# Linear attention's values and decayed keys: block transposes on VectorE and transfers through device memory in the place of 64 TensorE transposes

## The chip, the cores and the metric

The kernel runs on one core of a Trainium2 chip, as one program from its first instruction to its last. The metric is the device time of one execution in microseconds. A core has a matrix engine (TensorE, PE in the profile), a vector engine (VectorE, DVE), a scalar engine (ScalarE, ACT), GpSimd (POOL) and SyncE (SP), which here only issues transfers. The engines work side by side, each through its own list in order, and wait for each other through semaphores. TensorE writes its results to PSUM, from where another engine fetches them.

## The reference

One step of a decoder layer for 256 tokens of a prompt and 8 x 4 tokens of samples, 288 in all, in float32. The layer projects the normalized input, runs two branches of attention, merges them, and ends with a feed-forward part:

```python
h = rms_norm(x, norm1)
z = h @ w_in                      # all projections in one
qs, ks, vs, qg, kg, vg, rg, ag, gs, gg = split(z)
o_swa = sliding_window_attention(...)
o_g, S_new = gla_recurrent(qg * 256 ** -0.5, kg, vg, log_a, S0)
o_g = o_g * rsqrt(mean(o_g * o_g) + EPS) * gla_norm * silu(rg)
y = sigmoid(gs) * (o_swa @ p_swa) + sigmoid(gg) * (o_g @ p_gla)
x = x + y @ w_o
x = x + square(relu(rms_norm(x, norm2) @ w_up)) @ w_down
```

What matters here is the linear attention `gla_recurrent`: 4 heads, keys of 256 features, values of 512. With the running sum `b` of the logarithm of the forget gates inside a chunk of tokens,

```python
q_i, k_i, k_d = q * exp(b), k * exp(-b), k * exp(b_last - b)
o = causal(q_i @ k_i.T) @ v + q_i @ S
S = exp(b_last) * S + k_d.T @ v
```

The state `S` of each head (256 x 512) is an output, one for the prompt and one for each of the 8 samples.

## The kernel before

Activations lie with features on the 128 partitions and the 288 tokens along the free axis. A projection is done by `gemm` (L220 to L253): weights come in chunks of 512 KB (`raw`, 6 buffers, loaded by SP at L231), ScalarE casts each half to a reduced float (`whi`, L216), VectorE takes the rest (`wlo`, by the helper at L156), 5 buffers each, and TensorE does 24 matmuls for each chunk (L249): hi by hi, hi by lo and lo by hi. 520 chunks follow each other in the order of `ORDER`.

Everything else is laid into this stream in small steps. `gla(h)` and `gla_sample(h)` are generators, put into two queues by `start_head(h)`; after each chunk `pump` takes some steps from each queue (rates 1.0 or 0.9, and 0.7). A `yield` ends a step. The written order is only a priority: a planner lays the instructions of each engine out by the times that it models, and keeps the written order where `keep_in_program_order` asks for it. On the chip each engine then works through its list strictly in order, SP's list of transfers too.

A head's projections `qk{h}` and `v{h}` fill `zqk[h]` and `zv[h]` (features on partitions). For the products with tokens as the summed axis, values and decayed keys are needed the other way round, tokens on partitions. `gla(h)` does this on TensorE:

- values of the prompt: for each of 2 blocks of 128 tokens, 4 transposes of 128x128 into the PSUM bank `pv` (L679) and a copy by ScalarE into `vt` (tile `vtok`, L680). From `vt` come `vh` and `vl`, the halves of the split values, which enter the products for the output (`po`, L806 to L809) and the state (`pst`, L823 to L826).
- decayed keys: `kd` for each half `t` of the 256 features (L725 is the last of its operations), then 2 x 2 transposes into the bank `pk` (L778), a cast by ScalarE into `kdt` (L779) and the remainders `kdl` by VectorE. They enter the state's products.
- the state's products of the last head are done at the end of the kernel from `vt` and `kdt`, which are kept till then.

`gla_sample(h)` turns the 32 tokens of the samples: 4 transposes into `pvs` (L840), a copy into `vf` (L841) and a write of `vf` to the device memory `vd` (L842). `vf` is used in products of the samples' output (L885); `vd` is read back much later by `state_updates`, broadcast to all partitions (`vb`, L1035). Between these steps `gla_sample` loads the samples' old states, 4 and then 4 more, into buffers of the same pool `raw` as the weights (L867), and multiplies them (`pos`, L892).

That makes 8 + 4 + 4 = 16 transposes for each head, 64 in all, in groups of four.

The tile pools matter for the order: tiles with the same tag share their buffers, and a new one waits until the readers of the old are done. `vt` shares its tag with `w2r`, the small weights that the head loads at its start (L655); `kdl` shares with `kd`, `kdt` with a part of the gates (tag B); tag F holds the tiles `ob` and `sqo` of `gla_sample`; the tags `Za0` to `Zb3` of the pool `main` hold the large tiles of the heads.

Of the kernel before, what the change touches and what calls it, by code (L numbers as in the profile page):

```python
# [12 lines left out]
F32 = mybir.dt.float32  # L13
# [6 lines left out]
P = 128  # L20
D = 2048
KT = 16
TP = 256
NB = 8
NS = 4
TS = NB * NS
NT = TP + TS
# [7 lines left out]
QS, KS, VS_, QG, KG, VG, RG, AG, GS, GG = OFF[:10]  # L35


def w_in_groups():

    ar = np.arange  # L40
    g = {}
    g["kv"] = np.concatenate([ar(KS, KS + 256), ar(VS_, VS_ + 256)])
    for p in range(2):
        cols = []
        for r in range(4):
            for u in range(2):
                h = (2 * p + u) * 4 + r
                cols.append(ar(QS + h * 64, QS + h * 64 + 64))
        g[f"q{p}"] = np.concatenate(cols)
    for i in range(4):  # L50
        g[f"gs{i}"] = ar(GS + i * 512, GS + i * 512 + 512)
        g[f"gg{i}"] = ar(GG + i * 512, GG + i * 512 + 512)
        g[f"rg{i}"] = ar(RG + i * 512, RG + i * 512 + 512)
        g[f"qk{i}"] = np.concatenate([ar(QG + i * 256, QG + i * 256 + 256), ar(KG + i * 256, KG + i * 256 + 256)])
        g[f"v{i}"] = ar(VG + i * 512, VG + i * 512 + 512)
    return g


def swa_rows():

    rows = []
    for p in range(2):
        for r in range(4):
            for u in range(2):
                h = (2 * p + u) * 4 + r
                rows.append(np.arange(h * 64, h * 64 + 64))
    return np.concatenate(rows)
# [64 lines left out]
def step_kernel(ctx: ExitStack, tc: tile.TileContext, a: dict):  # L132
# [7 lines left out]
    def f(ap):  # L140
        return ap.bitcast(F32)

    def bank(name):
        return psm.tile([P, 512], F32, name=name, tag="sm")

    def flat(ap):
        return ap.rearrange("p a b -> p (a b)")
# [7 lines left out]
    def sub(out, x, y, eng=V):  # L155
        eng.tensor_tensor(out, x, y, ALU.subtract)  # L156


    ident = main.tile([P, P], F32, name="ident")
# [472 lines left out]

    dec = gpool.tile([P, 4, 2, NB], F32, name="dec")
    kdk = gpool.tile([P, 4, 2, TS], F32, name="kdk")
    vd = ctx.enter_context(tc.tile_pool(name="values", bufs=1, space=bass.MemoryType.DRAM)).tile([4, TS, 512], F32, name="vd")
    V.memset(qm, 0.0)
    wsel, wsgn = bm[:, 64 + NB:65 + NB], bm[:, 65 + NB:66 + NB]

# [10 lines left out]

    def gla(h):  # L650
        zq, zk = (lambda t: zqk[h][:, t]), (lambda t: zqk[h][:, 2 + t])
        yield
        w2r = gpool.tile([P, 256], F32, name="w2r", tag="vtok")
        w2 = gpool.tile([P, 256], F32R, name="w2")
# [19 lines left out]

        vt = gpool.tile([P, 2, 512], F32, name="vtok", tag="vtok")
        for blk in range(2):
            pv = bank("pv")
            for j in range(4):
                T.transpose(pv[:, P * j:P * j + P], zv[h][:, j, P * blk:P * blk + P], ident)  # L679
            S.copy(vt[:, blk], pv)  # L680
            yield
        o_g = og[h] = main.tile([P, 4, NT], F32, name=f"og{h}", tag=f"Zb{h}")

        kds, ee, ees = [], [], []
        for t in range(2):
            e = main.tile([P, 9, P], F32, name="e", tag=f"Za{2 + t}")
            en = gpool.tile([P, 2, P], F32, name="en", tag="en", bufs=2)
            kd = gpool.tile([P, 2, P], F32, name="kd", tag="kd", bufs=2)
            tot = gpool.tile([P, 1], F32, name="tot", tag="tot", bufs=2)
            cs = gpool.tile([P, 2, 6], F32, name="cs", tag="cs", bufs=2)  # L690

            px = pfx[:, t, 0:TP].rearrange("p (a b c) -> p a b c", a=2, c=32)
            end = px[:, :, :, 31]

            add(cs[:, :, 0:5:4], end[:, :, 0:4:2], end[:, :, 1:4:2])
            V.tensor_copy(cs[:, :, 1:6:4], end[:, :, 1:4:2])
            add(cs[:, :, 2:4], cs[:, :, 0:2], cs[:, :, 4:5].broadcast_to([P, 2, 2]))
            S.activation(tot, cs[:, 1, 2:3], AF.Exp, scale=GATE)
            runs = lambda i: e[:, i:i + 2].rearrange("p a (b c) -> p a b c", c=32)
            far, l64, dg, l32 = runs(0), runs(2), runs(4), runs(7)  # L700
            sub(far, cs[:, :, 2:6].unsqueeze(3).broadcast_to([P, 2, 4, 32]), px)
            sub(l64[:, :, 0:2], cs[:, :, 0:2].unsqueeze(3).broadcast_to([P, 2, 2, 32]), px[:, :, 0:2])
            V.tensor_copy(l64[:, :, 2], px[:, :, 2])
            add(l64[:, :, 3], px[:, :, 3], end[:, :, 2:3].broadcast_to([P, 2, 32]))
            yield
            sub(dg, px, px[:, :, :, 15:16].broadcast_to([P, 2, 4, 32]))
            sub(l32[:, :, 0:4:2], end[:, :, 0:4:2].unsqueeze(3).broadcast_to([P, 2, 2, 32]), px[:, :, 0:4:2])
            V.tensor_copy(l32[:, :, 1:4:2], px[:, :, 1:4:2])
            running(e[:, 6], ones, las[t][:, P:TP])
            S.activation(flat(en), flat(e[:, 4:6]), AF.Exp, scale=-GATE)  # L710
            S.activation(flat(e), flat(e), AF.Exp, scale=GATE)
            yield
            q2 = zq(t)[:, 0:TP].rearrange("p (a b) -> p a b", a=2)
            k2 = zk(t)[:, 0:TP].rearrange("p (a b) -> p a b", a=2)
            mul(e[:, 0], e[:, 0], k2[:, 0])
            mul(e[:, 6], e[:, 6], q2[:, 1])
            mul(e[:, 2:4, 0:64], e[:, 2:4, 0:64], k2[:, :, 0:64])
            mul(e[:, 2:4, 64:P], e[:, 2:4, 64:P], q2[:, :, 64:P])
            for i, x in ((0, k2), (32, q2)):
                e5 = e[:, 7:9].rearrange("p a (b c) -> p a b c", b=2)[:, :, :, i:i + 32]  # L720
                mul(e5, e5, x.rearrange("p a (b c) -> p a b c", b=2)[:, :, :, i:i + 32])
            mul(e[:, 4:6], e[:, 4:6], q2)
            mul(en, en, k2)
            mul(kd[:, 1], e[:, 1], k2[:, 1])
            V.tensor_scalar(kd[:, 0], e[:, 0], tot, None, ALU.mult)  # L725
            kds.append(kd)
            yield
            ee.append(e)
            ees.append(en)
        pa = bank("pa")  # L730
        V.memset(pa[:, :448], 0.0)

# [39 lines left out]
        yield  # L772
        parts = h < 3
        kdt = gpool.tile([P, 2, 256], F32R if parts else F32, name="kdt", tag="B")
        pk = bank("pk")
        for blk in range(2):
            for t in range(2):
                T.transpose(pk[:, 256 * blk + P * t:256 * blk + P * t + P], kds[t][:, blk], ident)  # L778
        S.copy(flat(kdt), pk)  # L779
        if parts:  # L780
            kdl = [gpool.tile([P, 256], F32R, name="kdl", tag="kd", bufs=2) for _ in range(2)]
            for blk in range(2):
                sub(kdl[blk], pk[:, 256 * blk:256 * blk + 256], f(kdt[:, blk]))
            vh = main.tile([P, 2, 512], F32R, name="vh", tag="tt")
            vl = []
            for blk in range(2):
                S.copy(vh[:, blk], vt[:, blk])
                for c in (slice(0, 256), slice(256, 512)):
                    lo = main.tile([P, 256], F32R, name="vl", tag=("zr", "sr")[blk], bufs=2)
                    sub(lo, vt[:, blk, c], f(vh[:, blk, c]))  # L790
                    vl.append(lo)
                yield
            ath, atl = (gpool.tile([P, 256], F32R, name=n) for n in ("ath", "atl"))
            S.copy(ath, at[0])
            sub(atl, at[0], f(ath))
            yield
# [35 lines left out]
    def gla_sample(h):  # L832
# [2 lines left out]
        ps = ready[h][:, :, TP:NT]  # L835

        vf = gpool.tile([TS, 512], F32, name="vf")
        pv = bank("pvs")
        for j in range(4):
            T.transpose(pv[:TS, P * j:P * j + P], zv[h][:, j, TP:NT], ident)  # L840
        S.copy(vf, pv[:TS])  # L841
        SY.dma_start(vd[h], vf)  # L842
        yield
        ps4 = ps.rearrange("p a (b c) -> p a b c", c=NS)
        es = gpool.tile([P, 2, 64], F32, name="es")
# [183 lines left out]
    def state_updates():  # L1029
# [2 lines left out]

        def load_values(i):
            h, b = items[i]
            SY.dma_start(vb[:, i % 2], vd[h, 4 * b:4 * b + 4].rearrange("a b -> (a b)").unsqueeze(0).broadcast_to([P, 2048]))  # L1035
        load_values(0)

        paced = tc.keep_in_program_order
# [128 lines left out]
def lay_out(i):  # L1167
# [3 lines left out]
    m["x"] = np.ascontiguousarray(x.T.reshape(KT, P, NT).transpose(1, 0, 2))  # L1171
    feat = lambda v: v.reshape(-1, P).T
    m["xn"] = np.concatenate([feat(i["norm1"][0]), m["x"][:, 0]], axis=1)
    m["norms"] = np.concatenate([feat(i["norm2"][0]), feat(i["final_norm"]), feat(i["gla_norm"][0])], axis=1)
    w_in = i["w_in"][0]
    parts = {n: pack(w_in[:, c])[0] for n, c in w_in_groups().items()}
    for n, w in (("ps", i["p_swa"][0][swa_rows()]), ("pg", i["p_gla"][0]), ("wo", i["w_o"][0])):
        p = pack(w)
        for j in range(4):
            parts[f"{n}{j}"] = p[j]  # L1180
# [13 lines left out]
    ck, cv = i["cache_swa_k"][0], i["cache_swa_v"][0]  # L1194
    m["kc"] = np.ascontiguousarray(ck.reshape(NB, P, 2, P).transpose(2, 3, 0, 1))
    m["vc"] = np.ascontiguousarray(cv.reshape(NB, P, 2, P).transpose(2, 1, 0, 3))
    s0 = i["state_gla"][0]
    m["s0"] = np.ascontiguousarray(s0.reshape(NB, 4, 2, P, 512).transpose(1, 0, 3, 2, 4)).reshape(4, NB, P, 1024)
    return {k: np.ascontiguousarray(v) for k, v in m.items()}

# [38 lines left out]
```

## Time and profile before

| | us |
|---|---|
| median of 3 runs | 1745.99 |
| lowest and highest run | 1745.26, 1748.83 |
| span of the profiled execution, first to last instruction | 1748.4 |
| weight chunks: TensorE's time for 24 matmuls, from the chain | 3.15 to 3.17 |
| transposes of the change: first and last start | 223.7, 633.6 |

The profile gives no other time of its own execution than the span, which lies within those of the three runs. A line of the groups names the line of the program, the engine, the operation, the tiles (result, then operands), the shapes and the count; behind the bar stand the busy time of all, the mean length of one in ns, and the time that the engine was idle just before them, with those who ended that wait. The chain is followed back from the last instruction, at each step to what released it or to the instruction before it on its engine. "SPq" is SP's own list of transfers.

### The profile page before, as it was taken

The numbers are of one execution on the slowest core, as the hardware profiler recorded it, in microseconds if no ns is written. First come the engines' busy times: TensorE is split into PE (matmuls) and PEld (weight loads), VectorE is DVE, ScalarE is ACT, GpSimd is POOL, SyncE is SP. The second block draws the span as 40 slices with busy tenths as digits, with TensorE's granted clock in tenths as the row PEclk, the third lists the DMA queues.
The fourth block names the chain that finished last, engine by engine and source line by source line (L and its number), as shares of the span: only waits on it lengthen the run. The fifth ranks groups of instructions, "written<-read, shape, count | busy, mean of one in ns | idle before, by whom it ended". The sixth has DMA issues, their size and how long they took to land.

```text
span 1748.4 us, 34547 instructions
## 1 busy us (share of the span) xinstructions
PE 1737.7 (99%) x13491; PEld 1710.8 (98%) x13491; DVE 1207.2 (69%) x2312; ACT 890.9 (51%) x1681; POOL 2.9 (0%) x12
## 2 busy tenths in 40 slices
PE   9999999999999999999999999999999999999997
PEld 8999999999999999999999999999999999999997
DVE  8896575665745656666678777777777777777555
ACT  6555465444534645544556554455544554455543
POOL 0000000000000000000000000000000000000000
PEclk9999999999999999999999999999999999999999
DMA  8645456456464465555866677776777677765552
GB/s 302 212 138 181 136 171 220 169 191 208 158 246 159 147 229 169 185 167 166 320 217 235 235 268 252 275 255 249 255 247 283 239 240 281 267 240 210 176 178 92
DMA packets 102883, 374.74 MB, mean 214 GB/s; under 512 B 12480, under 2 KB 15040, under 8 KB 98624
## 3 DMA queue, kind: packets, MB, share of 16 engines
q1 hardware_dynamic: 102144, 371.49, 60.5%
q8 instruction: 105, 1.72, 0.4%
q10 hardware_dynamic: 576, 1.05, 0.2%
q14 instruction: 58, 0.48, 0.1%
HBM read 348.58 MB, written 23.92 MB: 213 GB/s over the span
## 4 chain that ended last, share of the span: by engine, by line
PE 99%; DVE 0%; DMA 0%; ACT 0%; issue 0%; DVEq 0%
PE mm L249 94%; PE pos L892 1%; PE score L458 0%; PE o L502 0%; PE pt L490 0%; PE po L806 0%; PE os L582 0%; DVE x L150 0%; PE po L809 0%; DMA raw<-in_w 0%; PE pv L679 0%; PE pa L734 0%; PE pst L825 0%; PE pst L823 0%; PE pst L826 0%; PE ssq L258 0%
## 5 line engine op out<-in xcount | busy, mean ns | idle before, releaser
L156 DVE TENSOR_TENSOR wlo<-raw,whi 128x512 fp32r<-128x512 f32 x1040 | 703.0, 688 | 455.3 <-ACT whi L216 449.8
L216 ACT CAST whi<-raw 128x512 fp32r<-128x512 f32 x1040 | 630.8, 619 | 721.1 <-PE mm L249 660.9
L249 PE MATMUL mm<-hh,whi 128*128 128x288 f32 x1472 | 436.3, 297 | 0.1
L249 PE MATMUL mm<-hl,whi 128*128 128x288 f32 x1472 | 431.4, 294 | 0.0
L249 PE MATMUL mm<-hh,wlo 128*128 128x288 f32 x1472 | 429.4, 292 | 0.0
L249 PE MATMUL mm<-uh,whi 128*128 128x288 f32 x1024 | 301.1, 294 | 0.0
L249 PE MATMUL mm<-ul,whi 128*128 128x288 f32 x1024 | 301.1, 294 | 0.0
L249 PE MATMUL mm<-h2h,whi 128*128 128x288 f32 x1024 | 301.1, 294 | 0.0
L249 PE MATMUL mm<-h2l,whi 128*128 128x288 f32 x1024 | 301.1, 294 | 0.0
L249 PE MATMUL mm<-uh,wlo 128*128 128x288 f32 x1024 | 300.7, 294 | 0.0
L249 PE MATMUL mm<-h2h,wlo 128*128 128x288 f32 x1024 | 300.7, 294 | 0.0
L249 PEld LDWEIGHTS mm<-hh,whi 128*128 128x128 f32 x1472 | 276.2, 188 | 5.9 <-issue 3.0
L249 PEld LDWEIGHTS mm<-hl,whi 128*128 128x128 f32 x1472 | 276.1, 188 | 0.3
L249 PEld LDWEIGHTS mm<-hh,wlo 128*128 128x128 f32 x1472 | 276.0, 188 | 0.0
L249 PEld LDWEIGHTS mm<-uh,wlo 128*128 128x128 f32 x1024 | 193.2, 189 | 0.0
L249 PEld LDWEIGHTS mm<-h2h,wlo 128*128 128x128 f32 x1024 | 193.2, 189 | 0.0
L249 PEld LDWEIGHTS mm<-uh,whi 128*128 128x128 f32 x1024 | 192.4, 188 | 0.0
L249 PEld LDWEIGHTS mm<-h2h,whi 128*128 128x128 f32 x1024 | 192.4, 188 | 0.0
L249 PEld LDWEIGHTS mm<-h2l,whi 128*128 128x128 f32 x1024 | 191.8, 187 | 0.0
L249 PEld LDWEIGHTS mm<-ul,whi 128*128 128x128 f32 x1024 | 191.8, 187 | 0.0
L1047 DVE SCALAR_TENSOR_TENSOR acc_s<-vb,kdk,acc_s 128x512 f32<-128x512 f32 x192 | 142.2, 745 | 0.4
L249 PE MATMUL mm<-yl,whi 128*128 128x288 f32 x256 | 75.2, 294 | 0.0
(290 smaller groups left out, 1778.1 us busy)
## 6 DMA issues: line engine op xcount, KB each, us to landing
raw<-in_w SPq DMA_DIRECT2D x518, 512.0 KB, 3.9
vb<-vd SPq DMA_DIRECT2D x32, 1024.0 KB, 6.9
raw<-in_s SPq DMA_DIRECT2D x32, 512.0 KB, 4.2
old<-in_s SPq DMA_DIRECT2D x32, 512.0 KB, 4.2
out_ssn<-old SPq DMA_DIRECT2D x32, 512.0 KB, 5.2
x<-in_x SPq DMA_DIRECT2D x4, 576.0 KB, 6.5
x<-in_x SPq DMA_DIRECT2D x6, 288.0 KB, 7.1
out_y<-x SPq DMA_DIRECT2D x6, 288.0 KB, 2.7
```

The lines of the kernel that those rows point to most:

```text
L156: eng.tensor_tensor(out, x, y, ALU.subtract)
L216: S.copy(hi, raw)
L249: T.matmul(o, lhsT=(lo if j == 2 else hi)[:, sl], rhs=xl(k) if j == 1 else xh(k), start=k == 0 and j == 0, stop=k == nk - 1 and j == 2)
L892: T.matmul(pos[r:r + 32], lhsT=qm[:, t, 32 * b:32 * b + 32], rhs=st[i + g][:, 512 * t:512 * t + 512], start=b < 2, stop=b >= NB - 2)
L1047: paced(V.scalar_tensor_tensor(acc[t], v(n), k(n), acc[t], ALU.mult, ALU.add))
```

## The change

Each head's values and decayed keys are turned by VectorE in blocks of 32x32. Such an operation turns each block in its place, so that a tile of 128 features by 288 tokens becomes, in each group of 32 partitions, 9 blocks of 32 tokens by 32 features. The groups are put together by writes to device memory: the group of 32 partitions `g` writes its features into its own columns, and reading back rows of tokens gives tokens on partitions.

- `gla(h)` has a new first step: four block transposes into `vtb` (in the buffer `Za2`), four writes of the samples' block to `vd[h]` and four of the prompt's eight blocks to `vtd[h]`. In the place of transposes and copies, two loads fill `vt` from `vtd[h]`.
- for each half `t` of the keys a block transpose goes into `ktb` (tag F), then four writes to `kdd[h]`. Later two loads fetch the turned keys: for the first three heads into the two tiles `kdl`, from which, one step later, ScalarE casts `kdt` and VectorE takes the remainder in place; for the last head directly into `kdt`.
- `gla_sample(h)` loads `vf` from `vd[h]`; its transposes, the copy and the write of `vf` go.
- the features of a head come in another order this way (`VALUES`, `KEYS`). The gate's columns `rg`, the rows of `p_gla`, `gla_norm` and the old states are laid out in that order on the host, and the states are put back in the old order on the host when the kernel is done.

```diff
+def blocks_turned(n):
+    return np.arange(32 * 4 * n).reshape(n, 4, 32).transpose(1, 0, 2).ravel()
+VALUES, KEYS = blocks_turned(4), blocks_turned(2)
...
-        g[f"rg{i}"] = ar(RG + i * 512, RG + i * 512 + 512)
+        g[f"rg{i}"] = RG + i * 512 + VALUES
...
-    vd = ctx.enter_context(tc.tile_pool(name="values", bufs=1, space=bass.MemoryType.DRAM)).tile([4, TS, 512], F32, name="vd")
+    dram = ctx.enter_context(tc.tile_pool(name="values", bufs=1, space=bass.MemoryType.DRAM))
+    vd = [dram.tile([TS, 512], F32, name=f"vd{h}") for h in range(4)]
+    vtd = [dram.tile([NB, 32, 512], F32, name=f"vtd{h}") for h in range(4)]
+    kdd = [dram.tile([NB, 32, 256], F32, name=f"kdd{h}") for h in range(4)]
...
     def gla(h):
         zq, zk = (lambda t: zqk[h][:, t]), (lambda t: zqk[h][:, 2 + t])
+        yield
+        vtb = main.tile([P, 9, 4, 32], F32, name="vtb", tag="Za2")
+        for m in range(4):
+            V.transpose(vtb[:, :, m], zv[h][:, m].rearrange("p (t c) -> p t c", c=32))
+        for g in range(4):
+            rows_ = vtb[32 * g:32 * g + 32].rearrange("p t m c -> p t (m c)")
+            cols = slice(P * g, P * g + P)
+            SY.dma_start(vd[h][:, cols], rows_[:, 8])
+            SY.dma_start(vtd[h][:, :, cols].rearrange("t a x -> a t x"), rows_[:, 0:8])
         yield
...
         for blk in range(2):
-            pv = bank("pv")
-            for j in range(4):
-                T.transpose(pv[:, P * j:P * j + P], zv[h][:, j, P * blk:P * blk + P], ident)
-            S.copy(vt[:, blk], pv)
+            SY.dma_start(vt[:, blk], vtd[h][4 * blk:4 * blk + 4].rearrange("t a x -> (t a) x"))
             yield
...
-        kds, ee, ees = [], [], []
+        ee, ees = [], []
+        ktb = gpool.tile([P, NB, 2, 32], F32, name="ktb", tag="F")
...
-            kds.append(kd)
+            V.transpose(ktb[:, :, t], flat(kd).rearrange("p (b c) -> p b c", c=32))
             yield
             ee.append(e)
             ees.append(en)
+        for g in range(4):
+            SY.dma_start(kdd[h][:, :, 64 * g:64 * g + 64].rearrange("t a x -> a t x"),
+                         ktb[32 * g:32 * g + 32].rearrange("p b t c -> p b (t c)"))
...
-        pk = bank("pk")
-        for blk in range(2):
-            for t in range(2):
-                T.transpose(pk[:, 256 * blk + P * t:256 * blk + P * t + P], kds[t][:, blk], ident)
-        S.copy(flat(kdt), pk)
         if parts:
             kdl = [gpool.tile([P, 256], F32R, name="kdl", tag="kd", bufs=2) for _ in range(2)]
+        for blk in range(2):
+            SY.dma_start(f(kdl[blk]) if parts else kdt[:, blk], kdd[h][4 * blk:4 * blk + 4].rearrange("t a x -> (t a) x"))
+        if parts:
+            yield
             for blk in range(2):
-                sub(kdl[blk], pk[:, 256 * blk:256 * blk + 256], f(kdt[:, blk]))
+                S.copy(kdt[:, blk], f(kdl[blk]))
+                sub(kdl[blk], f(kdl[blk]), f(kdt[:, blk]))
...
         vf = gpool.tile([TS, 512], F32, name="vf")
-        pv = bank("pvs")
-        for j in range(4):
-            T.transpose(pv[:TS, P * j:P * j + P], zv[h][:, j, TP:NT], ident)
-        S.copy(vf, pv[:TS])
-        SY.dma_start(vd[h], vf)
+        SY.dma_start(vf, vd[h])
...
-            SY.dma_start(vb[:, i % 2], vd[h, 4 * b:4 * b + 4].rearrange("a b -> (a b)").unsqueeze(0).broadcast_to([P, 2048]))
+            SY.dma_start(vb[:, i % 2], vd[h][4 * b:4 * b + 4].rearrange("a b -> (a b)").unsqueeze(0).broadcast_to([P, 2048]))
```

More of the change, by code (lines that the diff above doesn't have):

```diff
@@ L1173, in lay_out @@
     m["xn"] = np.concatenate([feat(i["norm1"][0]), m["x"][:, 0]], axis=1)
-    m["norms"] = np.concatenate([feat(i["norm2"][0]), feat(i["final_norm"]), feat(i["gla_norm"][0])], axis=1)
+    m["norms"] = np.concatenate([feat(i["norm2"][0]), feat(i["final_norm"]), feat(i["gla_norm"][0][VALUES])], axis=1)
     w_in = i["w_in"][0]
     parts = {n: pack(w_in[:, c])[0] for n, c in w_in_groups().items()}
-    for n, w in (("ps", i["p_swa"][0][swa_rows()]), ("pg", i["p_gla"][0]), ("wo", i["w_o"][0])):
+    for n, w in (("ps", i["p_swa"][0][swa_rows()]), ("pg", i["p_gla"][0].reshape(4, 512, D)[:, VALUES].reshape(D, D)), ("wo", i["w_o"][0])):
         p = pack(w)
@@ L1196, in lay_out @@
     m["vc"] = np.ascontiguousarray(cv.reshape(NB, P, 2, P).transpose(2, 1, 0, 3))
-    s0 = i["state_gla"][0]
+    s0 = i["state_gla"][0][..., VALUES]
     m["s0"] = np.ascontiguousarray(s0.reshape(NB, 4, 2, P, 512).transpose(1, 0, 3, 2, 4)).reshape(4, NB, P, 1024)
@@ L1231 @@
     vc = o["vcn"].transpose(2, 1, 0, 3).reshape(NB, P, 4, 64)
-    sp = o["sp"].reshape(1, 1, 4, 256, 512)
-    ss = o["ssn"].reshape(4, NB, P, 2, 512).transpose(1, 0, 3, 2, 4).reshape(1, NB, 4, 256, 512)
+    vo, ko = np.argsort(VALUES), np.argsort(KEYS)
+    sp = o["sp"].reshape(1, 1, 4, 256, 512)[:, :, :, ko][..., vo]
+    ss = o["ssn"].reshape(4, NB, P, 2, 512).transpose(1, 0, 3, 2, 4).reshape(1, NB, 4, 256, 512)[..., vo]
     c = np.ascontiguousarray
```

## The prediction

> **What bounds the kernel now.** I read the page first: the busy time of each engine and the chain of work that ended last.
>
> ```profile
> PE 1737.7 (99%) x13491; PEld 1710.8 (98%) x13491; DVE 1207.2 (69%) x2312; ACT 890.9 (51%) x1681; POOL 2.9 (0%) x12
> ...
> PE 99%; DVE 0%; DMA 0%; ACT 0%; issue 0%; DVEq 0%
> ```
>
> TensorE (PE) is busy 99% of the span and 99% of the chain is TensorE. So the end comes when TensorE's list is worked off: what leaves that list shortens the run, and what is added elsewhere costs only where it makes TensorE wait. The average hides stages, so next come the busy times in the four stretches in which the four heads of the linear attention run beside the projections (columns: stretch, its length, busy time and instructions of PE, PEld, DVE, ACT, POOL, then granted clock, DMA share, GB/s).
>
> ```profile
> 205.00:315.00 110.00, 110.00 (x907) 105.17 (x906) 64.91 (x150) 58.82 (x106) 0.70 (x2) 1.00 0.53 187
> 315.00:430.00 115.00, 115.00 (x930) 111.03 (x930) 72.83 (x165) 54.50 (x103) 0.66 (x2) 1.00 0.55 188
> 430.00:545.00 115.00, 115.00 (x935) 111.03 (x935) 69.45 (x156) 53.41 (x100) 0.66 (x2) 1.00 0.55 190
> 545.00:660.00 115.00, 115.00 (x933) 111.19 (x932) 70.08 (x156) 59.77 (x109) 0.66 (x2) 1.00 0.54 187
> ```
>
> All 64 transposes of the change lie in these stretches. TensorE has no gap in any of them, VectorE (DVE) is idle 42 to 46 us of each, ScalarE (ACT) 51 to 62 us, and the transfers use some 55% of the DMA engines. Busy time alone would mislead, because matmuls overlap. What a transpose takes from the chain is read in the chain itself, here between 205 and 330 us, head 0 (start, length, what, how many):
>
> ```profile
> 223.84 0.44 PE pvs L840 x4
> ...
> 236.89 0.44 PE pv L679 x4
> ...
> 276.25 0.44 PE pk L778 x4
> ...
> 278.89 12.80 PE mm L249 x96
> ```
>
> Four transposes stand together each time, and each group holds the chain for 0.44 us, whichever of the three kinds it is. A head has four such groups: one `pvs`, two `pv`, one `pk`.
>
> **The change part by part.** The groups by line hold what goes, the nearest relatives of what comes, and the two steps that prepare the weights (after the count: busy in all, mean ns of one, idle time before and who ended it):
>
> ```profile
> L156 DVE TENSOR_TENSOR wlo<-raw,whi 128x512 fp32r<-128x512 f32 x1040 | 703.0, 688 | 455.3 <-ACT whi L216 449.8 <-PE pk L778 3.9
> L216 ACT CAST whi<-raw 128x512 fp32r<-128x512 f32 x1040 | 630.8, 619 | 721.1 <-PE mm L249 660.9 <-DMA raw<-in_w 38.3 <-ACT whi L216 8.5
> ...
> L249 PEld LDWEIGHTS mm<-hh,whi 128*128 128x128 f32 x1472 | 276.2, 188 | 5.9 <-issue 3.0 <-ACT whi L216 1.6 <-ACT kdt L779 0.8
> ...
> L648 DVE TENSOR_TENSOR_SCAN pfx<-seg,ls 128x288 f32<-128x288 f32 x8 | 5.6, 739 | 0.0
> ...
> L679 PE MATMUL pv<-ident,zv 128*128 128x128 f32 x32 | 4.8, 272 | 0.0
> ...
> L396 DVE STREAM_SHUFFLE rot<-swa_q 128x288 f32<-128x288 f32 x8 | 3.6, 480 | 0.0
> ...
> L840 PE MATMUL pvs<-ident,zv 128*32 128x128 f32 x16 | 2.4, 272 | 0.0
> L778 PE MATMUL pk<-ident,kd 128*128 128x128 f32 x16 | 2.4, 272 | 0.0
> ```
>
> *TensorE.* 32 + 16 + 16 = 64 transposes in 16 groups. At 0.44 us each they give back **16 x 0.44 = 7.0 us**. The 272 ns of one in its row is its length from start to end; on the chain four follow each other 0.11 us apart, so the rows' 64 x 0.272 = 17.4 us is an upper end that I don't take. The Trainium skill, page "TensorE: Matmul & The Clock Gate", Part 4, gives some 275 ns for a transpose inside a kernel: the trace's 272 ns agrees as a duration, but a sum of 64 such durations would promise 17.6 us where the chain shows 7.0.
>
> *ScalarE* loses the copies of the turned values out of PSUM, three in each head; for three heads the one cast of the keys becomes two of half its width, and the fourth head's goes. It is off the chain and idle almost half of each stretch: nothing either way.
>
> *VectorE* gains, for each head, four block transposes of 128x288 and two of 128x256. The trace of before has none. The nearest row is the shuffle of 128x288, 480 ns, which also moves elements between partitions; the scan of that size, 739 ns, is my upper end, and below nothing there is no reason to go. With 480 ns: 4 x 0.48 + 2 x 0.48 x 256/288 = 2.8 us a head, 11.1 us in all (17.1 by the scan). A burst of 1.9 us delays the `wlo` step that stands behind it. What hides this: VectorE is idle 455.3 us before those steps, mostly waiting for ScalarE's casts, and ScalarE's casts waited 660.9 us for TensorE to free a buffer. The preparation of weights runs ahead of TensorE, so I cost it at nothing; if the cover were gone, it would cost the 11.1 us.
>
> *SP's queue.* Per head come 8 writes of the turned values, 1 + 2 loads of them, 4 writes and 2 loads of the keys; the write of `vd` from `vf` goes: 16 more. Issue and landing times (first SP's own instructions with min/median/max ns, then KB each and median us to landing):
>
> ```profile
> L231 SPq DMA_DIRECT2D raw<-in_w x512: 327/328/1973, 18.0 to 1710.4; - x171
> ```
>
> ```profile
> raw<-in_w SPq DMA_DIRECT2D x518, 512.0 KB, 3.9
> vb<-vd SPq DMA_DIRECT2D x32, 1024.0 KB, 6.9
> ...
> w2r<-in_w SPq DMA_DIRECT2D x4, 128.0 KB, 2.7
> ...
> vd<-vf SPq DMA_DIRECT2D x4, 64.0 KB, 1.6
> ```
>
> 16 x 0.33 = 5.2 us of issuing in a head of 115 us. The bytes are small: per head about 0.6 MB of values and 0.25 MB of keys, written once and read once, against 512 KB for every single chunk of weights. What matters is order: SP works its list in sequence, and the new loads wait until the writes they read back have landed, while the weight loads stand behind them. Both waits are new, `vtd` to `vt` and `kdd` to `kdt`. SP's waits as they are (who for whom: us in total, times, longest):
>
> ```profile
> SPq L231 <- DVE wlo L156: 1069.6, 417, 8.4
> ```
>
> SP spends 1069.6 us waiting for a free weight buffer, so weights are normally asked for as early as the buffers allow. The values have time: they are written when the head begins and their first use in `vh` lies several chunks later. The thin place is behind the second four state loads. There (SP, ScalarE and VectorE in order of time, head 0: start, length, what):
>
> ```profile
> 267.86 28.62 SPq L231 DMA_DIRECT2D raw<-in_w  x13
> ```
>
> ```profile
> 275.87 1.90 ACT L216 CAST whi<-raw 128x512 fp32r<-128x512 f32 x3 [2.92 <-DMA raw<-in_w]
> ```
>
> ```profile
> 276.52 1.97 DVE L156 TENSOR_TENSOR wlo<-raw,whi 128x512 fp32r<-128x512 f32 x3 [5.47 <-ACT whi L216]
> ```
>
> A load issued at 267.86 is cast at 275.87; its first `wlo` part is done at 276.52 + 0.69 = 277.2, and the chain above begins with these weights at 278.89. The cover is 1.7 us, and 1.2 us once the `pk` group is out of the way. I take the same cover for the other heads. If the keys' loads were late just here, ScalarE's new copy of `kdl` would hold the casts behind it. The price per head is the landing less 1.2 us: 2.7 - 1.2 = 1.5 us by the load of the same 128 KB (`w2r`), 3.9 - 1.2 = 2.7 us by a weight load; three heads have that copy, so 0 to 8.1 us. Below nothing: the 0.8 us for which TensorE waited on `kdt` may go. Which end is nearer follows from when the keys are ready:
>
> ```profile
> 245.07 0.28 DVE L725 TENSOR_SCALAR kd<-e,tot 128x128 f32<-128x128 f32 x1
> ```
>
> I take **+0.5 us**, near the lower end, since in head 0 the last product that is turned ends at 245.35, about 30 us before this place: the two block transposes and the landings of the write and the load (1.6 and 2.7 us) fit in between.
>
> The extra steps of the head's list (one at its start, one after the keys' loads) move its work by a chunk; TensorE has projections to do meanwhile: nothing.
>
> **The sum.** -7.0 + 0.5 = -6.5 us, 0.37%. The profiled span is 1748.4 us, within the runs (1745.26 to 1748.83) and 2.4 above their median; I take the difference over to the median: 1745.99 - 6.5 = **1739.5 us**. About 0.2%, 3.5 us, is what a measurement of this kernel can tell from no change, so faster means below 1742.5 and slower above 1749.5.
>
> **The rivals.**
> - *Given back at the landings* (the same): the copy of `kdl` waits in ScalarE's order at the thin place. With 1.5 us in three heads 1745.99 - 7.0 + 4.5 = 1743.5, with 2.7 us 1747.0. For it: the cast there already waits 2.92 us for a transfer. Against it: the keys are early in head 0.
> - *SP holds the weights back* (slower): the keys' loads stand in SP's list ahead of weight loads at the thin place, and SP waits for the landing of `kdd`. By the only read-back that the trace has, 6.9 us, it costs 4 x (6.9 - 1.2) = 22.8 us: 1761.8. It decides from 10.5 us lost in all, that is a hold of 2.6 + 1.2 = 3.8 us in each head. Against it: the 1069.6 us show SP ahead of the work, waiting for buffers far more than for results, and the keys' loads can be asked for while it waits for one.
> - *VectorE becomes the bound* (slower): its 11.1 us land on the path: 1745.99 - 7.0 + 11.1 = 1750.1. Against it: 42 us idle in each stretch. The Trainium skill, page "VectorE: DVE Perf Modes", section "Rules for kernel authors", advises TensorE for a 128x128 transpose whose result may go to PSUM, which speaks against the change; it goes by the single operation, and the rows say which engine has time to spare.
> - *Full durations are saved* (faster): 1745.99 - 17.4 = 1728.6. Against it: the 0.44 us of each group in the chain.
> - *The change doesn't shorten TensorE's run* (the same): the transposes filled time in which weights were not ready, and TensorE now waits instead: 1746. Against it: only 5.9 us of idle time before the largest group of weight loads in 1472 of them.
>
> **Chances.** Forecast 0.68; given back 0.18; SP holds back 0.08; VectorE 0.02; full durations 0.02; no shorter 0.02. So faster 0.68 + 0.02 = 0.70, the same 0.18 + 0.02 = 0.20, slower 0.08 + 0.02 = 0.10. The range: at the low end the full 7.0 us and the 0.8 us of waiting, from the fastest run, 1745.26 - 7.8 = 1737.5, rounded down to 1737.0; at the top the dearer form of the first rival, 1747.0, rounded up to 1747.5. That leaves out the last slower and faster cases, some 0.12, and a little of the forecast's edges.
>
> **What the profile after would show.** Right: no `pv`, `pvs` and `pk` groups; some 64 fewer TensorE instructions, no new piece in the chain in their place; block transposes near 0.48 us with VectorE's busy time up by some 11 us; ScalarE's some us lower; the idle time before `mm` weight loads as small as now. Wrong: `mm` loads that wait for `whi` or `wlo` right after the keys' loads (first two rivals), or SP's waits on `vtd` or `kdd` of over 4 us each with weight loads behind them.

## The result, and the profile after

| | us |
|---|---|
| before, median of 4 runs (lowest, highest) | 1746.56 (1745.26, 1748.83) |
| changed, median of 4 runs (lowest, highest) | 1739.91 (1738.3, 1740.5) |
| ratio, with its 95% interval | 0.9961 (0.9949 to 0.9972) |
| profiled execution of the changed kernel: time, span | 1738.3, 1736.6 |

The change takes 6.65 us off, 0.38%. The page of the changed kernel, busy times and shares of the chain:

```profile
PE 1725.7 (99%) x13427; PEld 1699.0 (98%) x13427; DVE 1213.8 (70%) x2336; ACT 884.7 (51%) x1671; POOL 2.9 (0%) x12
...
PE 99%; DVE 1%; DMA 0%; ACT 0%; issue 0%; DVEq 0%
```

13491 - 13427 = 64 instructions have left TensorE, and 99% of the chain is still TensorE. That fits a run that got shorter because TensorE's list did; the experiments have to show it. The four stretches of the heads, in the columns of the prediction:

```profile
205.00:315.00 110.00, 110.00 (x904) 105.42 (x903) 67.22 (x158) 58.06 (x105) 0.72 (x2) 1.00 0.60 203
315.00:430.00 115.00, 115.00 (x927) 111.11 (x927) 74.80 (x171) 53.12 (x100) 0.65 (x2) 1.00 0.62 208
430.00:545.00 115.00, 115.00 (x933) 111.11 (x933) 71.90 (x164) 53.36 (x101) 0.65 (x2) 1.00 0.61 205
545.00:660.00 115.00, 115.00 (x932) 111.26 (x931) 73.46 (x163) 58.84 (x106) 0.66 (x2) 1.00 0.62 206
```

TensorE has no gap in any of them. VectorE is busy 2 to 3 us more in each, and the transfers use 60 to 62% of the DMA engines where they used 53 to 55%. The chain in head 0, at the places where the groups `pvs`, `pv` and `pk` stood:

```profile
210.78 15.75 PE mm L257 x120
226.53 0.26 PE pl L686 x2
226.79 37.83 PE mm L257 x288
...
268.45 9.45 PE mm L257 x72
277.90 0.35 PE pos L902 x8
278.25 1.85 PE pos L909 x16
280.10 12.79 PE mm L257 x96
292.89 0.44 PE pt L920 x4
```

No group of the change is left and no wait stands in its place; the 0.44 us at 292.89 are a group that the change doesn't touch (the samples' output). The groups by line of what came, and of the preparation of weights (busy in all, mean ns of one, idle time before):

```profile
L164 DVE TENSOR_TENSOR wlo<-raw,whi 128x512 fp32r<-128x512 f32 x1040 | 703.3, 688 | 443.5 <-ACT whi L224 440.8
...
L257 PEld LDWEIGHTS mm<-hh,whi 128*128 128x128 f32 x1472 | 275.8, 188 | 6.0 <-issue 4.7
```

```profile
L666 DVE STREAM_TRANSPOSE vtb<-zv 128x288 f32<-128x288 f32 x16 | 6.3, 447 | 0.0
...
L744 DVE STREAM_TRANSPOSE ktb<-kd 128x256 f32<-128x256 f32 x8 | 3.5, 434 | 0.0
```

24 block transposes take 6.3 + 3.5 = 9.8 us of VectorE. The page's total rises by 6.6, since an instruction's time overlaps its neighbours' there (four of 447 ns take 1.55 us in head 0). The `wlo` steps still wait 443.5 us for their casts, 12 us less than before, and the idle time before the largest group of weight loads is 6.0 us where it was 5.9. ScalarE's busy time falls by 6.2 us. The new transfers (KB each, median us to landing), and SP's waits (for whom: us in total, times, longest):

```profile
vtd<-vtb SPq DMA_DIRECT2D x16, 128.0 KB, 2.2
...
vtok<-vtd SPq DMA_DIRECT2D x8, 256.0 KB, 3.9
...
kdl<-kdd SPq DMA_DIRECT2D x6, 128.0 KB, 4.1
...
kdd<-ktb SPq DMA_DIRECT2D x16, 64.0 KB, 2.0
```

```profile
SPq L239 <- DVE wlo L164: 1012.8, 410, 6.8
...
SPq L697 <- DMA vtd<-vtb: 2.8, 4, 0.8
```

For the landing of `vtd` SP waits 0.8 us at most. The thin place of the prediction, ScalarE in head 0:

```profile
263.31 0.71 ACT L803 CAST kdt<-kdl 128x256 fp32r<-128x256 f32 x2
...
276.39 2.40 ACT L224 CAST whi<-raw 128x512 fp32r<-128x512 f32 x4 [4.65 <-PE mm L257]
```

The copy of the keys comes 13 us ahead of the weight cast that it might have held up, and that cast now waits for TensorE to free a buffer, not for a transfer.

**Where the two traces part.** A mark that both have is the first product with the weights of `p_gla`, right after the last head's projections (the tile `gh`: min/median/max ns, first to last start). Before, and changed:

```profile
L249 PE MATMUL mm<-gh,whi x256: 289/293/397, 722.3 to 822.8; 128*128 128x288 f32 x128
```

```profile
L257 PE MATMUL mm<-gh,whi x256: 291/293/399, 715.0 to 815.5; 128*128 128x288 f32 x128
```

At this mark, when the last of the 64 transposes is long past, the changed kernel is 7.3 us ahead. A little of that is older than the heads. The tile `ot` is written by four transposes that stand in all these kernels right before the heads' work, before and changed:

```profile
L589 PE MATMUL ot<-ident,ov x4: 270/272/272, 210.4 to 210.7; 128*128 128x128 f32 x4
```

```profile
L597 PE MATMUL ot<-ident,ov x4: 270/272/272, 210.2 to 210.5; 128*128 128x128 f32 x4
```

From the first of them to the mark it takes 722.3 - 210.4 = 511.9 us before and 715.0 - 210.2 = 504.8 after, 7.1 less. In three profiled executions of the changed kernel this stretch takes 504.8 to 505.0 us, while the mark itself moves by 0.5 (714.9 to 715.4), because the executions don't start alike.

The spans differ by more, 1748.4 - 1736.6 = 11.8 us. The other 4.5 arise after the mark, where both kernels do the same, and a second profiled execution of the changed kernel shows that they don't belong to the change: from the mark to the end it takes 1026.1 us, as long as before, where the first took 1021.6. First the execution above, then the other one (`after_again`), the products with `uh` in the feed-forward part, up to 1600 us:

```profile
L257 PE MATMUL mm<-uh,wlo x768: 287/291/297, 1017.9 to 1520.9; 128*128 128x288 f32 x192
```

```profile
L257 PE MATMUL mm<-uh,wlo x768: 291/295/295, 1018.2 to 1524.2; 128*128 128x288 f32 x192
```

503.0 us in one execution and 506.0 in the other, with the same instructions; the span of the other is 1741.0. In the profile of before the stretch takes 505.9 (1025.7 to 1531.6). So the traces are compared by the stretch from `ot` to the mark, the kernels by the medians of their runs.

### The profile page after: what moved, and what is told of

The parts are those of the page before. It is cut to its first block, busy times and chain, and to the rows that moved or that the text cites. A ratio compares the mean times of both kernels' runs of the same rounds, so it can differ in the third digit from the quotient of the medians.

```text
span 1736.6 us, 34533 instructions
## 1 busy us (share of the span) xinstructions
PE 1725.7 (99%) x13427; PEld 1699.0 (98%) x13427; DVE 1213.8 (70%) x2336; ACT 884.7 (51%) x1671; POOL 2.9 (0%) x12
## 4 chain that ended last, share of the span: by engine, by line
PE 99%; DVE 1%; DMA 0%; ACT 0%; issue 0%; DVEq 0%
PE mm L257 94%; PE pos L909 1%; PE score L466 0%; PE o L510 0%; PE pt L498 0%; PE po L827 0%; PE os L590 0%; DVE x L158 0%; DMA raw<-in_w 0%; PE po L830 0%; PE pa L755 0%; PE pst L846 0%; PE pst L844 0%; PE pst L847 0%; PE ssq L266 0%; PE scs L554 0%
## 5 line engine op out<-in xcount | busy, mean ns | idle before, releaser
L164 DVE TENSOR_TENSOR wlo<-raw,whi 128x512 fp32r<-128x512 f32 x1040 | 703.3, 688 | 443.5 <-ACT whi L224 440.8
L257 PE MATMUL mm<-gh,whi 128*128 128x288 f32 x256 | 75.2, 294 | 0.0
## 6 DMA issues: line engine op xcount, KB each, us to landing
raw<-in_w SPq DMA_DIRECT2D x518, 512.0 KB, 4.1
raw<-in_s SPq DMA_DIRECT2D x32, 512.0 KB, 4.3
old<-in_s SPq DMA_DIRECT2D x32, 512.0 KB, 4.6
out_ssn<-old SPq DMA_DIRECT2D x32, 512.0 KB, 4.6
```

What stands on the lines that cost most here:

```text
L257: T.matmul(o, lhsT=(lo if j == 2 else hi)[:, sl], rhs=xl(k) if j == 1 else xh(k), start=k == 0 and j == 0, stop=k == nk - 1 and j == 2)
```

## The experiments

The theory: TensorE's list sets the time, each group of four transposes is worth 0.44 us of it, and all that came in its place runs beside it. The rivals are those of the prediction. All kernels but the repeats and `e2_keys` are edits of the changed one. Each time stands beside runs of before on the same chip, whose medians lie between 1746.07 and 1747.48; the mark is the first start in the row of `gh`, and "heads" is the time from the first start in the row of `ot` to the mark.

| run | median us | ratio to before (95%) | mark us | heads us |
|---|---|---|---|---|
| before (mark: its profile above) | 1746.27 (21 runs) | | 722.3 | 511.9 |
| after_again: changed kernel | 1738.83 | 0.9948 (0.9934 to 0.9962) | 714.9 | 505.0 |
| e1_values | 1740.75 | 0.9961 (0.9949 to 0.9974) | 717.3 | 507.0 |
| e2_keys | 1743.81 | 0.9982 (0.9973 to 0.9990) | 720.1 | 510.1 |
| e3_unread | 1745.61 | 0.9993 (0.9984 to 1.0002) | 722.3 | 512.0 |
| e4_thrice | 1739.19 | 0.9954 (0.9941 to 0.9966) | 715.9 | 505.7 |
| e5_nowait | 1739.01 | 0.9955 (0.9943 to 0.9967) | 715.1 | 504.8 |
| e6_late | 1739.60 | 0.9956 (0.9944 to 0.9968) | 715.4 | 505.3 |
| e7_probs | 1746.35 | 0.9995 (0.9986 to 1.0004) | 721.9 | 505.0 |
| e8_out | 1738.18 | 0.9952 (0.9939 to 0.9964) | 715.1 | 503.2 |
| e10_seven | 1762.23 | 1.0086 (1.0073 to 1.0100) | 737.5 | 527.3 |
| after_beside: changed kernel | 1738.81 | 0.9955 (0.9938 to 0.9972) | 715.4 | 504.8 |
| e8_again | 1736.41 | 0.9935 (0.9921 to 0.9949) | 713.3 | 503.0 |

### The changed kernel again

> The changed kernel itself, beside the kernel before on one chip. Theory (TensorE's list is the run; 16 groups of four transposes at 0.44 us leave it and nothing is given back): 7.0 us under the kernel before, ratio 0.9960. Rival (a part of the measured gain is chance of the run): anything between 0.997 and 0.999. In the trace the first matmul of the products with p_gla, which come after all four heads, starts 7 us earlier than in the kernel before by the theory.

1738.83 us, 7.4 below before beside it, the mark at 714.9, and 505.0 us for the heads, 6.9 less than before.

### Values alone, keys alone

Each kernel keeps one half of the change and does the other as before. `e1_values` has the `pk` transposes and the copy of `kdt` from PSUM again:

```diff
-            V.transpose(ktb[:, :, t], flat(kd).rearrange("p (b c) -> p b c", c=32))
+            kds.append(kd)
...
+        pk = bank("pk")
         for blk in range(2):
-            SY.dma_start(f(kdl[blk]) if parts else kdt[:, blk], kdd[h][4 * blk:4 * blk + 4].rearrange("t a x -> (t a) x"))
+            for t in range(2):
+                T.transpose(pk[:, 256 * blk + P * t:256 * blk + P * t + P], kds[t][:, blk], ident)
+        S.copy(flat(kdt), pk)
```

> Only the values go by VectorE and device memory; the decayed keys are turned by TensorE as before. Theory: 12 of 16 groups leave TensorE's list, 12 x 0.44 = 5.3 us under the kernel before, ratio 0.9970. Rival (the waits for the keys' landings give back a part): this version has no such waits and would be as fast as the full change or faster, 7 us or more under the kernel before. Rival (the relief of ScalarE and of the PSUM banks is what counts): three of the four copies per head go, also 5.3 us, so this run does not tell that one apart.

`e2_keys` was made from the kernel before, with the keys' part of the change put in. Beside the changed kernel it has `pv` and `pvs` again, and the values in their old order; the edit of `pv`:

```diff
-            SY.dma_start(vt[:, blk], vtd[h][4 * blk:4 * blk + 4].rearrange("t a x -> (t a) x"))
+            pv = bank("pv")
+            for j in range(4):
+                T.transpose(pv[:, P * j:P * j + P], zv[h][:, j, P * blk:P * blk + P], ident)
+            S.copy(vt[:, blk], pv)
```

> Only the decayed keys go by VectorE and device memory; the values are turned by TensorE as before. Theory: 4 of 16 groups leave TensorE's list, 1.8 us under the kernel before, ratio 0.9990. Rival (the waits for the keys' landings give back a part): no gain or a loss, 1.000 or above.

Values: 5.5 us off the median and 511.9 - 507.0 = 4.9 off the heads, 0.41 for each of 12 groups. Keys: 2.5 and 1.8, 0.45 for each of 4. Each half pays by the number of its groups, near the 0.44 of the chain, and 4.9 + 1.8 = 6.7 us make up nearly all of the 7.

### The transposes put back, with nobody to read them

```diff
             V.transpose(vtb[:, :, m], zv[h][:, m].rearrange("p (t c) -> p t c", c=32))
+        for _ in range(3):
+            pv = bank("unread")
+            for j in range(4):
+                T.transpose(pv[:, P * j:P * j + P], zv[h][:, j, 0:P], ident)
...
             V.transpose(ktb[:, :, t], flat(kd).rearrange("p (b c) -> p b c", c=32))
+            pv = bank("unread")
+            for j in range(2):
+                T.transpose(pv[:, P * j:P * j + P], kd[:, j], ident)
```

> The changed kernel, to which 64 TensorE transposes are added (12 after the block transposes of the values in each head, 2 behind each of the two of the keys) whose results nobody reads. Theory: TensorE's list is as long as before, so 6.6 to 7.0 us over the changed kernel and within 0.4 us of the kernel before, ratio 0.9997 to 1.000. Rival (the copies that ScalarE lost, the PSUM banks' readers or the shorter way of the values brought the gain): those stay away here, so the run stays near the changed kernel, ratio 0.996.

The row of the mark in this kernel:

```profile
L257 PE MATMUL mm<-gh,whi x256: 289/293/401, 722.3 to 822.8; 128*128 128x288 f32 x128
```

It is back at the place of before, the heads take 512.0 us against 511.9, and the median is 1745.61 - 1738.83 = 6.8 us above the changed kernel's. All that the change added and all that it took from ScalarE and the PSUM banks is still so in this kernel; only the 64 transposes are back, and they cost the whole gain. It is 0.11 us for each, not the 0.272 of its duration: with that, it would have been 17.4.

### VectorE's part three and seven times

```diff
-            V.transpose(vtb[:, :, m], zv[h][:, m].rearrange("p (t c) -> p t c", c=32))
+            for _ in range(3):
+                V.transpose(vtb[:, :, m], zv[h][:, m].rearrange("p (t c) -> p t c", c=32))
...
-            V.transpose(ktb[:, :, t], flat(kd).rearrange("p (b c) -> p b c", c=32))
+            for _ in range(3):
+                V.transpose(ktb[:, :, t], flat(kd).rearrange("p (b c) -> p b c", c=32))
```

> The changed kernel with each of the 24 block transposes of VectorE done three times into the same place, 48 more of 0.435 us by the trace of the changed kernel, 20.9 us of VectorE in all. Theory (VectorE's idle time and the five weight buffers hide them): no more than 1 us over the changed kernel, ratio to before 0.996, and the first matmul with p_gla within 1 us of 714.9 us. Rival (VectorE becomes the bound in the stretches of the heads): up to 20.9 us over the changed kernel, ratio up to 1.008.

`e10_seven` is the same with 7.

> The changed kernel with each of the 24 block transposes done seven times into the same place. In each head 28 stand in one piece at its start, 28 x 0.37 = 10.4 us by the trace of the run with three. Theory (what hides VectorE's work is the lead of the weights over TensorE, 4.9 us in the middle, and not VectorE's idle time, of which there are over 40 us in each stretch): 10.4 - 4.9 = 5.5 us lost in each head, 22 us in all, the first matmul with p_gla near 737 us. Rival (idle time of the stretch is what counts): 7 x 10.4 us of VectorE fit into 4 x 42 us, so within 2 us of 714.9 us.

Three times over costs 0.7 to 0.9 us in the heads and nothing that the medians can tell. Seven times costs 22.4 us in the heads, 5.6 in each. The chain of `e10_seven` at the start of head 1, and VectorE there:

```profile
324.56 6.18 PE mm L257 x47
...
334.74 0.60 DVE wlo L164
335.33 8.01 DVE vtb L667 x23
343.34 0.21 issue
343.56 0.43 DVE vtb L667
343.99 0.59 DVE wlo L164
...
344.62 7.51 PE mm L257 x43
```

```profile
335.25 8.74 DVE L667 STREAM_TRANSPOSE vtb<-zv 128x288 f32<-128x288 f32 x24
343.92 0.65 DVE L164 TENSOR_TENSOR wlo<-raw,whi 128x512 fp32r<-128x512 f32 x1
```

TensorE waits four times for the `wlo` behind such a burst, once in each head (who for whom: us, times, longest):

```profile
PE mm L257 <- DVE wlo L164: 14.9, 4, 4.9
```

Here is what the cover is: not the 42 us that VectorE is idle in a stretch, but how far the prepared weights are ahead of TensorE, since the `wlo` behind the burst waits for all of it. In head 1 the last `wlo` ahead of the burst is done at 335.33 us, and TensorE starts again at 344.62 after a wait of 2.9, so the weights that were ready kept it going for some 6.4 us. The same working gives 5.8 to 6.7 us for the four heads. The length of a burst sorts the three kernels: 1.55 us in the changed one hides; 12 transposes, 4.4 us in head 0, let TensorE wait nowhere and cost some 0.2 in a head; 28, some 10 us, stop it for 2.6 to 4.9 us.

The waits are 14.9 of the 22.4 us. The other 7.5 come after them: the 43 matmuls behind the burst of head 1 take 0.175 us each, the 47 at 324.56 took 0.131. Worked out so for all four bursts, it makes 7.7 us. The granted clock was 0.55 from 346 to 348 us and 0.60 from 348 to 350, and 1.00 from 350 on; behind the other three bursts it was 0.50 for a time too. So the forecast of 22 us was met in part by luck: its lead of 4.9 us was too short, which made the stops too long, and it had no term for the slower clock.

### No wait for the landings

Heads 1 to 3 load what the head before them wrote, which has landed long since; only head 0 still reads its own. The turned values and keys that enter the products of heads 1 to 3 are thus those of the head before. The last head writes into the memory of the first.

```diff
-            SY.dma_start(vt[:, blk], vtd[h][4 * blk:4 * blk + 4].rearrange("t a x -> (t a) x"))
+            SY.dma_start(vt[:, blk], vtd[max(h - 1, 0)][4 * blk:4 * blk + 4].rearrange("t a x -> (t a) x"))
```

and the same for the loads of the keys and of `vf`; the writes go to `vtd[h % 3]` and `kdd[h % 3]`.

> The changed kernel, but from the second head on the loads of turned values and keys fetch what the head before has written, which landed long ago: as many transfers, no wait of a load for a landing. What is computed of heads 2 to 4 from turned values and keys belongs to other heads. Theory (those waits cost nothing): the first matmul with p_gla within 0.5 us of 714.9 us, ratio to before 0.996. Rival (a part is given back at the landings): earlier than 714.9 by what they cost, 1.5 to 8 us.

SP waits for the landing of `vtd` once (0.7 us) where it waited four times (2.8 us). The heads take 504.8 us against 504.8 to 505.0: with the landings of three heads taken out of the way, nothing is won. They cost nothing that this measure can tell.

### The keys written as late as can be

The four writes to `kdd[h]` stand directly before the loads that read them, and the `yield` behind the loads goes.

```diff
-        for g in range(4):
-            SY.dma_start(kdd[h][:, :, 64 * g:64 * g + 64].rearrange("t a x -> a t x"),
-                         ktb[32 * g:32 * g + 32].rearrange("p b t c -> p b (t c)"))
...
+        for g in range(4):
+            SY.dma_start(kdd[h][:, :, 64 * g:64 * g + 64].rearrange("t a x -> a t x"),
+                         ktb[32 * g:32 * g + 32].rearrange("p b t c -> p b (t c)"))
         for blk in range(2):
             SY.dma_start(f(kdl[blk]) if parts else kdt[:, blk], kdd[h][4 * blk:4 * blk + 4].rearrange("t a x -> (t a) x"))
         if parts:
-            yield
```

> The changed kernel with the writes of the turned keys moved to directly before the loads that read them back, and without the step between the loads and ScalarE's cast of them, so that the whole way of write, landing, load, landing (2.0 + 4.1 us by the trace of the changed kernel) lies at the place where weights are scarcest. Theory (cover of 1.2 us there, the rest comes through): three heads x (6.1 - 1.2) = 14.7 us at the most, and some us at the least if the planner sets the casts behind other work; a start of the first matmul with p_gla between 716 and 730 us. Rival (the planner's order hides even this): within 1 us of 714.9 us.

My theory missed: the mark is at 715.4, and the heads take 505.3 us, some 0.4 more than in the changed kernel. SP now waits for the keys to land (who for whom: us, times, longest):

```profile
SPq L239 <- DVE wlo L164: 1005.7, 403, 6.8
...
SPq L799 <- DMA kdd<-ktb: 5.8, 4, 2.8
```

Four waits, 2.8 us at the longest, under the 3.8 from which the rival "SP holds the weights back" decides. What was lost from SP's other waits is of the same size, 1012.8 - 1005.7 = 7.1 us: that fits an SP that would have stood still for a free weight buffer in that time anyway. The written order is only a priority: in head 0 SP's list has the four writes between other loads from 251.1 to 258.7 us and the loads of the keys at 261.9, where the changed kernel starts its writes at 251.2 and its loads at 258.5. So the edit moved the keys by little, and what a copy at the thin place itself would cost, no run here shows.

### The same recipe where there is less room

The window attention of the prompt turns its probabilities by 48 TensorE transposes. This kernel does them in VectorE's blocks too, through device memory, besides the change; the loads and the products with the values each come one step later.

```diff
-            for u in range(2):
-                pt = bank("pt")
-                for i in range(3):
-                    T.transpose(pt[:, i * P:i * P + P], sc[:, u, i * P:i * P + P], ident)
-                S.copy(sts[:, u], pt[:, :384])
+            tb = pool.tile([P, 24, 32], F32, name="tb")
+            V.transpose(tb, flat(sc).rearrange("p (b c) -> p b c", c=32))
+            for g in range(4):
+                SY.dma_start(ptd[pr][:, :, 32 * g:32 * g + 32].rearrange("b k q -> k b q"), tb[32 * g:32 * g + 32])
...
```

> The changed kernel with the same recipe for the probabilities of the prompt's window attention: their 48 TensorE transposes, 8 groups of six at 0.66 us in the chain, go; instead 8 block transposes of 128x768 on VectorE (0.94 us each by the rate of the shorter ones), 4 writes and 1 load for each. Theory (what leaves TensorE's list shortens the run): 8 x 0.66 = 5.3 us under the changed kernel, ratio to before 0.993, with the first matmul with p_gla at 709.6 us. Rival (VectorE, 91% busy from 66 to 100 us in the changed kernel, becomes the bound there, or the products wait for landings): the gain is given back, 0 to 7.5 us over the theory.

The theory missed again: 1746.35 us, all that the change had gained is gone. The loss lies ahead of the heads, which take 505.0 us as in the changed kernel, while `ot` starts at 216.9 instead of 210.2. The rival had the direction, but its price was too low: the mark is 12.3 us over the theory's 709.6, where it said 7.5 at most. The stretch from 100 us on, first in the changed kernel, then in this one:

```profile
100.00:170.00 70.00, 70.00 (x557) 67.96 (x554) 53.05 (x139) 40.08 (x104) 0.00 (x0) 1.00 0.50 166
```

```profile
100.00:170.00 70.00, 62.96 (x480) 57.97 (x482) 55.76 (x142) 31.37 (x86) 0.00 (x0) 0.98 0.64 165
```

VectorE is busy 55.76 of 70 us, only 2.7 more than in the changed kernel, and TensorE stands still for 7. So it isn't VectorE's total that fails; TensorE waits for single results. The chain there, from the longest pieces:

```profile
131.76 0.81 DVE sc L491 x3
132.57 0.89 DVE tb L499
...
152.40 0.98 DVE tb L499
153.40 0.33 SPq L501
...
153.77 0.52 SPq L501
154.34 0.54 SPq L501
154.93 0.59 SPq L501
155.57 5.31 DMA raw<-in_w
```

Two rivals of the prediction stand on the chain: the steps of the softmax and the block transposes on VectorE (`sc`, `tb`), and SP, which issues four writes (L501) ahead of a weight load, whose 5.31 us then lie open. How much each of them takes I did not separate; the edit also left the tile `rot` one buffer in the place of two, and the granted clock fell here too (0.98 over the stretch, 0.64 from 134 to 138 us). The Trainium skill, page "VectorE: DVE Perf Modes", section "Rules for kernel authors", advises TensorE for a 128x128 transpose whose result may go to PSUM. Here the measured time goes with it (1746.35); in the heads it goes against it (1739.91 against 1746.56). What sets the two places apart is how soon the result is due and how full VectorE is; which of these decides is not shown.

### One more group in the heads

In the heads one more group can go the same way. The samples' output `pos` is turned straight out of PSUM by VectorE, in the place of the copy by ScalarE and the group `pt2`, one for each head:

```diff
-        S.copy(ob, pos)
+        for g in range(4):
+            V.transpose(ob[:, P * g:P * g + P].rearrange("p (j c) -> p j c", c=32),
+                        pos.rearrange("p (j g c) -> p g j c", j=4, g=4)[:, g])
+        for q in range(4):
+            SY.dma_start(obd[h][:, :, q].rearrange("g r x -> r g x"),
+                         ob[32 * q:32 * q + 32].rearrange("p (g x) -> p g x", g=4))
+        yield
+        yield
+        SY.dma_start(ob, obd[h].rearrange("g r q x -> (g r) (q x)"))
...
-        pt = bank("pt2")
-        for j in range(4):
-            T.transpose(pt[:, P * j:P * j + P], ob[:, P * j:P * j + P], ident)
-        V.tensor_reduce(o_g[:, :, TP:NT], pt.rearrange("p (a b c) -> p a c b", a=4, b=4), AX.X, ALU.add)
+        V.tensor_reduce(o_g[:, :, TP:NT], ob.rearrange("p (b a c) -> p a c b", a=4, b=4), AX.X, ALU.add)
```

> The changed kernel with the same recipe for the samples' output of the linear attention, the last four groups of four transposes in the stretches of the heads: VectorE turns the sums straight out of PSUM in blocks, 4 writes and 1 load place them. ScalarE's copy goes too. Theory (each group is worth its 0.44 us of TensorE's list, as nothing in these stretches is short): 4 x 0.44 = 1.8 us under the changed kernel, ratio to before 0.995 or less, and the first matmul with p_gla at 713.2 us. Rival (VectorE's bursts or the longer way of the samples make TensorE wait): at 714.9 us or later.

The median (0.9952 of before) can't be told from the repeat of the changed kernel (0.9948), and the mark, 715.1, looks like the rival's. But in the profiled execution TensorE had done 107 matmuls after 20 us where the changed kernel had done 119, and those 12, at 0.13 us, make it start 1.6 us late: `ot` starts at 211.9 instead of 210.2. The heads take 503.2 us, 1.6 to 1.8 less than in the changed kernel. The next two runs set both kernels side by side on one chip.

> The changed kernel once more, as the measure for the next run on the same chip: ratio to before 0.995 to 0.996, about 7 us under the kernel before.

> The version with the samples' output turned by VectorE as well, beside the changed kernel on one chip. Theory: 1.8 us under the changed kernel in the median, and 1.8 us less in the trace between the first projection of the heads and the first matmul with p_gla. Rival (a gain too small to keep): no difference in the median.

1736.41 against 1738.81, the mark at 713.3 against 715.4, and 503.0 us for the heads against 504.8. 4 x 0.44 = 1.8 us were due; 1.8 came in the heads and 2.4 in the medians, whose runs hardly overlap (1736.08 to 1738.53 against 1738.45 to 1744.83). This kernel stands at 0.9935 (0.9921 to 0.9949) of before.

## Why the prediction was right

**TensorE's list, -7.0 us: right.** 16 groups of 0.44 us from the chain are 7.0; the heads take 6.9 to 7.1 us less, and `e3_unread`, which puts only the transposes back, takes 512.0 us for them against 511.9 before. The rival of the full durations (17.4 us) falls with it, and so does the one by which TensorE would wait instead. What ScalarE lost and the added steps of the head's list are worth nothing, as I had said: both are as in the changed kernel there.

**VectorE, nothing: right, with the cover named too broadly.** The block transposes took 447 and 434 ns, against 480 and 427 by the nearest row, 9.8 us in all against 11.1. I named VectorE's idle time and the lead of the preparation together; `e10_seven` shows that the lead counts, since TensorE waits there though VectorE's idle time would hold all the added work.

**The landings, +0.5 us: mis-sized, they cost nothing.** `e5_nowait` puts the term at nothing, within the 0.2 us by which the stretch of the heads differs between executions. The trace of before shows a cover of 1.7 us behind the state loads, but the new copy was not put there: the planner laid it 13 us ahead in head 0. In `e6_late`, where the code asks for writes and loads back to back, the planner pulled the writes apart from the loads by itself, and the cost was 0.4 us. The bound of 8.1 us was far too wide, because it took a place in the code for a place in the run. Why the cast at 276 us now waits for a buffer rather than for a transfer was not followed up.

**SP's 5.2 us of issuing, nothing: right.** SP's waits for a free buffer fell from 1069.6 to 1012.8 us. The second wait that I expected, on `kdd`, shows only where the writes are moved late.

**The sum.** -7.0 with no landings is -7.0, which is what the heads show. The medians differ by -6.65 and, in the two repeats, by -7.4 and -8.7, whose intervals overlap. So it is luck that -6.65 lies closer to my -6.5 than to -7.0: half a microsecond is less than these medians can tell. One step of the bookkeeping was loose: I set the span of before (1748.4) beside the times of runs, though 1.7 us lie outside a span (1738.3 against 1736.6 after); with them that execution took some 1750.1, above the runs that I named. It changed nothing, as the difference went over to the median.

## What to carry to other kernels

On an engine whose list sets the time, price a removed operation by its share of the chain (here 0.44 us for four transposes), not by its duration. Work that is handed to another engine is hidden by how far that engine's next product is ahead of its reader (here some 6 us), so keep each burst below that lead and spread it; the engine's idle total says little. The same handing over lost in the window attention, where VectorE was busy for 76% of the stretch already and the result was due a step later; which of the two decided is open.

## What I had not expected of the hardware

A short stop of TensorE costs more than its length: after the waits of 2.6 to 4.9 us in `e10_seven` the granted clock was 0.5 to 0.6 for some 3 to 4 us, and the four stops of 14.9 us in all cost 22.4.

The products of the feed-forward part have two speeds, by execution: 131.9 ns a matmul in the profiles of before, `after_again` and `e10_seven`, 131.1 in those of the changed kernel and most others. From the mark to the end it makes 4.5 us (1021.6 against 1026.1), about as much as the runs of one kernel differ: those of before went from 1745.13 to 1750.27, those of the changed kernel from 1738.12 to 1742.7. What sets it stays open; the granted clocks of the first two executions of the changed kernel are 0.999 and 0.998, but `after_beside` has the faster step at 0.998.

VectorE's block transpose reads PSUM as well as its own memory, here 128x128 in 284 ns (`e8_again`), 128x288 in 447, 128x768 in 971.
